# A hybrid decoder layer on one core: the float32 products inside a scan chunk, issued by two column halves of the stationary block

## The chip, the cores and the metric

The kernel runs on one core of one Trainium2 chip. The metric is the device time of one execution in microseconds. Before the change it is 1580.88 us, the median of three runs (1580.54 to 1581.92). The input is float32 and the output must agree with a float32 reference, so nearly all large products are done as three float32r products of a high and a low part (in the code `mm3` and `steps3`), and some small ones directly in float32.

## The reference, cut to what matters

One layer over 1024 tokens with 1024 channels: RMSNorm, one input projection, then two token mixers side by side (differential attention with 8 heads, and a Mamba-2 scan, "SSD", with 32 heads in 4 groups of 8), gates, three output projections. The change is in the scan. Its chunked form, with chunks of L = 128 tokens, is

```
a_cum = cumsum(dt * A)                                   # per chunk and head
seg   = a_t[..., :, None] - a_t[..., None, :]
decay = exp(where(causal, seg, -inf))                    # l x s, zero for s > l
cb    = einsum('bclgn,bcsgn->bcgls', Cc, Bc)
y_diag = einsum('bcgjls,bcsgjp->bclgjp', cb[:, :, :, None] * decay, xdt)
...
y_off = einsum('bclgn,bcgjpn->bclgjp', Cc, prev) * exp(a_cum)[..., None]
y = (y_diag + y_off) ...
```

`y_diag` is the product in question: for each chunk (8), each group (4) and each head in the group (8) a 128 x 128 block `cb * decay` (l by s) times a 128 x 64 block `xdt` (s by head channel). That is 32 chunks-and-groups, with 8 small products each.

## The kernel before, in words

The program is written out by a planner. Generators (one per piece of work: a head's projection, an attention block, a scan chunk) are run by `Plan.run` in the order in which the planner's clock `pl.t` says that they are due; each emitted instruction moves that clock or an engine's clock by a modelled cost. `pl.t` is the clock of TensorE: `mm` (line 207) emits one matmul and adds its cost, `tp` (line 216) a transpose. So the order in which instructions stand on each engine's queue follows from those costs. Nothing is moved afterwards: the kernel is compiled with a manual schedule. Loads and stores all go through SyncE's queue (`load`, line 262).

The stages on TensorE, in order of time: the normalised input and the front projections with conv and gates (to about 580 us, the scan of group 0 and the start of group 1 among them), attention heads with their projections `pma`, scores `sc`, transposes `pa`, value products `av`, and the rest of the scan woven in, with the last gates `pg` behind them (to about 1276 us), then the output projections, which use a Strassen-like scheme on sums of blocks (`pz`, `py`, `px` with `wp`, and `fYc`, `fXc`, `fZc` in the front; the final `po..`).

One scan chunk is `ssd_chunk(g, c, ...)`, line 1506. In the parts that matter:

- `ab` is a 128 x 8 x 128 tile: for the 8 heads of the group the block decay, transposed (partition is s, column is l). `load_ab` (line 1477) loads the cumulated exponents by one DMA, masks them on GpSimd (line 1482) and exponentiates on ScalarE, eight instructions. There is one such buffer.
- `pc` is the 128 x 128 product of B and C (`cb`), line 1547. VectorE multiplies `ab` by it, line 1623.
- `xdt` is x times dt, made on GpSimd.
- `pO` holds the off-diagonal part in PSUM, made by three float32r products (line 1578) and scaled in place by VectorE; in the first chunk of a group there is none, and the tile is called `pD`.
- The loop at line 1640 then does the 8 products with `ab[:, j, :]` as the stationary operand and 64 columns of `xdt` as the moving one, accumulating onto `pO` (or writing `pD`).
- Then VectorE adds the skip term, multiplies by the gate, and so on to the store of the chunk's output.

A float32 product that is not a transpose stands in the trace as two pairs of a weight load and a matmul: the 8 products of a chunk are 16 weight loads (PEld) and 16 matmuls (PE). In this text these 16 pairs of one chunk are called a burst; there are 32 of them, 28 written to `pO` and 4 to `pD`.

Of the kernel before, what the change touches and what calls it, by code (L numbers as in the profile page):

```python
# [15 lines left out]
P = 128  # L16
# [129 lines left out]
def tile_hybrid_layer(ctx: ExitStack, tc: tile.TileContext, x, norm_w, w_in, q_norm_w, k_norm_w,  # L146
# [40 lines left out]
    def midt(shape=(P, 512), dt=F32, name="m"):  # L187
        return mid.tile(list(shape), dt, tag="b2", name=name)
# [7 lines left out]
    def trt(name):  # L196
        return ps_tr.tile([P, 512], F32, tag="tr", name=name)
# [9 lines left out]
    def mm(o, lhsT, rhs, start, stop, after=0.0, **kw):  # L207
        nc.tensor.matmul(o, lhsT=lhsT, rhs=rhs, start=start, stop=stop, **kw)  # L208
        n, m = rhs.free_size(), lhsT.free_size()
        if rhs.dtype == F32:  # L210
            c = max(4 * n / 2400, 0.215)
        else:
            c = max(n / 2400 + lag[0], 0.057 if m <= 64 else 0.107)
        pl.t = max(pl.t, after) + c
# [8 lines left out]
    def mm3(o, ah, al, bh, bl, first, last):  # L223
        mm(o, ah, bh, first, False)
        mm(o, ah, bl, False, False)
        mm(o, al, bh, False, last)
# [1245 lines left out]
    def ssd_core(g):  # L1472
        state = {"st": {}, "pre": {}, "n": 0, "did": set()}
        ssd_n[g] = state
        abs_ = {}

        def load_ab(c):
            k = yield from pl.get(abb)
            ab = bigt([P, GH, P], name=f"ab{g}{c}")
            t = load(ab, act_d[c, g * GH:(g + 1) * GH, :].partition_broadcast(P)) + 1.0  # L1480
            yield t
            nc.gpsimd.affine_select(out=ab, in_=ab, pattern=[[0, GH], [1, P]], compare_op=ALU.is_ge, fill=-1e30,  # L1482
                                    base=0, channel_multiplier=-1)
            t = pl.op("G", 1.06, t, True)
            yield t
            for j in range(GH):
                t = act(ab[:, j, :], ab[:, j, :], AF.Exp, t - HOP, bias=nac[:, c, g * GH + j:g * GH + j + 1])
            abs_[c] = (ab, k, t)
        need = [(b, h) for b in [16 + g, 20 + g] + list(range(g * 4, g * 4 + 4)) for h in range(2)]
        while any(cv_at.get(i, INF) > pl.t for i in need) or any(z_at.get((g, t), INF) > pl.t for t in range(NT)):  # L1490
            yield pl.t + 0.5
        pl.spawn(load_ab(0))
        for c in range(NT):
            if c + 1 < NT:
                pl.spawn(load_ab(c + 1))
            while c - state["n"] >= 2 or c and c - 1 not in state["did"]:
                yield pl.t + 0.2
            pl.spawn(ssd_chunk(g, c, state, abs_))
            yield pl.t + (PACE if bigs.avail(3) <= pl.t or 'setup' in ready else SLOW)
# [6 lines left out]
    def ssd_chunk(g, c, state, abs_):  # L1506
# [19 lines left out]
        kxdt, xdt = kxr, midt(name=f"xdt{g}{c}")  # L1526
# [93 lines left out]
        ab, kab, t_ab = abs_.pop(c)  # L1620
# [13 lines left out]
        if c:  # L1634
            pD, k, t1 = cell
            yield max(t1, pl.t)
        else:
            k = yield from pl.get(trs, first=True)
            pD = trt(f"pD{g}{c}")
        for j in range(GH):  # L1640
            mm(pD[:, j * 64:(j + 1) * 64], ab[:, j, :], xdt[:, j * 64:(j + 1) * 64], c == 0, True,
               skip_group_check=True)
        abb.give(kab, pl.t + 0.1)
        at = max(pe_done(), t_n)
        yield at
# [583 lines left out]
```

## Time and profile before

| | |
|---|---|
| median of three runs | 1580.88 us (1580.54 to 1581.92) |
| profiled execution: time | 1580.41 us |
| profiled execution: span from first to last instruction | 1578.7 us |
| TensorE busy, matmul / weight load | 1553.7 us (98%) / 1299.0 us (82%) |
| VectorE, ScalarE, GpSimd busy | 75%, 60%, 50% |
| mean granted TensorE clock | 0.998 |
| first and last burst of the kind that is changed | 310.4 us, 1073.7 us (first matmul) |

PE is the matmul side of TensorE, PEld its weight-load side. [...] In a row of a timeline the columns are the start, the length from the first start to the last end, the engine, line, operation, tiles, shapes and the count of merged records. "128\*64" is the stationary block, rows by columns; "128x512 f32" the moving operand. The 1.7 us between the span and the execution's time lie around the first and the last instruction.

### The profile page before, as it was taken

How to read it: one execution, taken by the hardware profiler on the slowest of the kernel's cores; microseconds unless marked ns; L12 is line 12 of the kernel's file. 1: busy time of each engine (PE TensorE's matmuls, PEld its weight loads, DVE VectorE, ACT ScalarE, POOL GpSimd, SP SyncE). 2: the span in 40 equal slices, each digit the busy share in tenths (PEclk: the TensorE clock that was granted, in tenths of full speed). 3: DMA queues.
4: the chain of work that ended last, by engine and by line, in shares of the span. 5: the costliest groups of instructions: out<-in, count | busy, mean ns of one | idle time of the engine just before them, and what ended most of it. 6: DMA issues, size and time to landing. Idle time of an engine off the chain costs nothing.

```text
span 1578.7 us, 24834 instructions
## 1 busy us (share of the span) xinstructions
PE 1553.7 (98%) x7858; PEld 1299.0 (82%) x7858; DVE 1183.6 (75%) x2143; ACT 939.4 (60%) x2273; POOL 785.3 (50%) x906
## 2 busy tenths in 40 slices
PE   7999999999999999999999999999999999999999
PEld 5777888888888888888888888888888888888887
DVE  6778867568787778767778787877556687898985
ACT  7653434467565576778677777776666554443350
POOL 3274465345555554546574846454756745332005
PEclk9999999999999999999999999999999999999999
DMA  6576698744454552424373522333336697798846
GB/s 227 162 250 194 230 301 284 247 153 139 133 150 157 151 158 96 134 62 122 111 236 122 152 89 81 110 112 118 107 134 224 193 366 253 267 323 273 302 140 220
DMA packets 254821, 287.38 MB, mean 182 GB/s; under 512 B 18391, under 2 KB 162528, under 8 KB 254690
## 3 DMA queue, kind: packets, MB, share of 16 engines
q1 hardware_dynamic: 254686, 285.79, 55.7%
q8 instruction: 62, 1.02, 0.3%
q14 instruction: 69, 0.57, 0.1%
q10 hardware_dynamic: 4, 0.00, 0.0%
HBM read 196.47 MB, written 89.26 MB: 181 GB/s over the span
## 4 chain that ended last, share of the span: by engine, by line
PE 85%; ACT 3%; DVE 3%; DMA 3%; POOL 3%; issue 2%; SPq 0%; POOLq 0%; DVEq 0%; ACTq 0%
PE pma L208 19%; PE pz L208 11%; PE py L208 5%; PE fYc L208 5%; PE sc L208 4%; PE pO L208 4%; PE av L208 4%; PE fXc L208 3%; PE fZc L208 3%; PE px L208 3%; PE fYg L208 3%; PE pg L208 2%; PE pmz L208 2%; PE pa L217 2%; PE poz L208 1%
## 5 line engine op out<-in xcount | busy, mean ns | idle before, releaser
L208 PE MATMUL pma<-w,hH 128*128 128x512 f32 x1024 | 343.8, 404 | 0.0
L208 PEld LDWEIGHTS pma<-w,hH 128*128 128x128 f32 x1024 | 187.7, 189 | 32.9 <-DVE xdt L242 0.2
L208 PE MATMUL pma<-w,hL 128*128 128x512 f32 x512 | 205.7, 402 | 0.0
L234 ACT ACTIVATE w<-raw 128x512 fp32r<-128x512 f32 (+1 forms) x166 | 101.3, 629 | 56.0 <-DMA raw<-wf_d 21.7
L242 DVE TENSOR_TENSOR w<-raw,w 128x512 fp32r<-128x512 f32 (+1 forms) x134 | 107.1, 817 | 27.0 <-ACT w L234 24.1
L234 ACT ACTIVATE p<-p,nm 128x256 f32<-128x256 f32 (+7 forms) x128 | 98.8, 774 | 33.8 <-DVE nm L916 33.3
L208 PEld LDWEIGHTS pma<-w,hL 128*128 128x128 f32 x512 | 96.5, 188 | 16.6
L242 POOL TENSOR_TENSOR rawf<-rawf,rawf 128x512 f32<-128x512 f32 x54 | 71.8, 1330 | 75.1 <-DVE wp L242 30.5
L208 PE MATMUL fYc<-ft,wp 128*128 128x512 f32 x432 | 106.5, 392 | 2.4 <-DVE ft L242 1.8
L208 PEld LDWEIGHTS fYc<-ft,wp 128*128 128x128 f32 x432 | 80.3, 188 | 20.2 <-DVE ft L242 2.2
L208 PE MATMUL pz<-w,ft 128*128 128x512 f32 x384 | 90.1, 391 | 0.9 <-DVE w L242 0.9
L234 ACT ACTIVATE wp<-rawp 128x512 fp32r<-128x512 f32 x72 | 44.1, 627 | 78.4 <-POOL rawp L242 25.6
L242 POOL TENSOR_TENSOR os<-os,os 128x512 f32<-128x512 f32 x48 | 66.9, 1393 | 36.4 <-DMA os<-in_w_in_dram 14.8
L208 PEld LDWEIGHTS pz<-w,ft 128*128 128x128 f32 x384 | 71.7, 188 | 16.0 <-DVE w L242 1.3
L242 POOL TENSOR_TENSOR rawp<-rawp,rawp 128x512 f32<-128x512 f32 x36 | 54.4, 1521 | 54.2 <-DVE wp L242 50.2
L234 ACT ACTIVATE ab<-ab,nac 128x128 f32<-128x128 f32 x256 | 78.5, 397 | 3.5 <-POOL ab L1482 3.4
L916 DVE CUSTOM_DVE_ANT_0 p<-sc,maskb 128x512 f32<-128x512 f32 (+3 forms) x128 | 72.4, 584 | 6.6 <-PE sc L208 6.0
L274 POOL TENSOR_TENSOR rs<-rs,mhalf 128x4 f32<-128x4 f32 (+1 forms) x71 | 72.8, 1025 | 5.9
L208 PE MATMUL av<-v,at 128*128 128x128 f32 x576 | 75.2, 275 | 0.0
L208 PEld LDWEIGHTS av<-v,at 128*128 128x128 f32 x576 | 72.5, 191 | 3.2
L234 ACT ACTIVATE wp<-rawf 128x512 fp32r<-128x512 f32 x100 | 60.5, 624 | 17.5 <-POOL rawf L242 16.3
L948 POOL TENSOR_TENSOR rec<-s,mone 128x1 f32<-128x1 f32 x64 | 37.2, 583 | 63.7 <-ACT p L234 62.5
(376 smaller groups left out, 4410.3 us busy)
## 6 DMA issues: line engine op xcount, KB each, us to landing
raw<-in_w_in_dram SPq DMA_DIRECT2D x104, 256.0 KB, 3.2
rawf<-in_w_in_dram SPq DMA_DIRECT2D x72, 256.0 KB, 4.7
ab<-act_d SPq DMA_DIRECT2D x32, 512.0 KB, 4.7
wf_d<-os SPq DMA_DIRECT2D x48, 256.0 KB, 5.1
cv_d<-cv SPq DMA_DIRECT2D x48, 256.0 KB, 2.9
raw<-wf_d SPq DMA_DIRECT2D x48, 256.0 KB, 3.3
t_d<-ts SPq DMA_DIRECT2D x24, 512.0 KB, 4.0
os<-in_w_in_dram SPq DMA_DIRECT2D x32, 256.0 KB, 3.8
```

Of the source, the lines that this page charges most:

```text
L208: nc.tensor.matmul(o, lhsT=lhsT, rhs=rhs, start=start, stop=stop, **kw)
L217: nc.tensor.transpose(out=o, in_=i, identity=ident if idn is None else idn)
L234: nc.scalar.activation(o, i, f, **kw)
L242: (nc.vector if eng == "V" else nc.gpsimd).tensor_tensor(out=o, in0=a, in1=b, op=op)
L274: nc.gpsimd.tensor_tensor(out=dst, in0=dst, in1=mhalf[:, 0:cols], op=ALU.pow)
L916: nc.vector.tensor_tensor_reduce(out=p[:, j:e], in0=sc[i][:, 0:e - j], in1=maskb[:, S - n + j:S - n + e], scale=-1.0, scalar=nms[i - 1] if ...
L948: nc.gpsimd.tensor_tensor(out=rec, in0=sums[1], in1=mone, op=ALU.pow)
```

## The change

Each head's 128 x 128 block goes to TensorE as two blocks of 128 x 64: columns 0 to 63 (the first 64 tokens of the chunk), whose result goes to PSUM partitions 0 to 63, and columns 64 to 127, whose result goes to partitions 64 to 127 of the same columns. The moving operand is the same 64 columns of `xdt` for both. Nothing is left out: the zero quarter of the first half (s > l) is still multiplied. In the built program each half occupies its own half of the array's columns: the first is placed at column 0, the second at column 64, each with a size of 128 rows by 64 columns. The planner's cost of a float32 product with a stationary block of at most 64 columns becomes 0.108 us, where a full one of 64 moving columns costs 0.215.

```
         n, m = rhs.free_size(), lhsT.free_size()
         if rhs.dtype == F32:
-            c = max(4 * n / 2400, 0.215)
+            c = max(4 * n / 2400, 0.215) if m > 64 else 0.108
         else:
...
         for j in range(GH):
-            mm(pD[:, j * 64:(j + 1) * 64], ab[:, j, :], xdt[:, j * 64:(j + 1) * 64], c == 0, True,
-               skip_group_check=True)
+            js = slice(j * 64, (j + 1) * 64)
+            for ls in (slice(0, 64), slice(64, P)):
+                mm(pD[ls, js], ab[:, j, ls], xdt[:, js], c == 0, True, skip_group_check=True)
```

The order on TensorE around the first burst of the program (group 0, chunk 0; `pz` is a product of the front's z projection), with the rows of before and of the change marked by - and +:

```order
 L208 MATMUL pz_2987<-w_2814,ft_335 128x512
 L208 MATMUL pz_2987<-w_2830,ft_333 128x512 x2
-L208 MATMUL pD_2996<-xdt_2855,ab_2795 128x64 x8
+L208 MATMUL pD_2996<-xdt_2855,ab_2795 64x64 x16
 L208 MATMUL pz_2987<-w_2830,ft_335 128x512
 L208 MATMUL pz_2987<-w_2868,ft_334 128x512 x2
```

Eight products become sixteen, each with an output of 64 partitions by 64 columns; the neighbours are the same. So it is at all 24 bursts of groups 0 to 2, and the other rows of TensorE stand as before up to 896 us in the trace of before (the transposes `py26` of group 2, chunk 6).

The planner's clock for a burst moves from 8 x 0.215 = 1.720 to 16 x 0.108 = 1.728 us. From there on that is enough to let work fall due in another order. TensorE before, around the first burst of group 3 (`pD30`; `pma43` is a projection of head 4, token block 3; `px31` is the next chunk's transposes):

```order
L217 MATMUL px31_10080<-ident_99,xr31_10012 128x128 x4
L208 MATMUL pma43_10067<-w117_9664,hH_114 128x512 x2
L208 MATMUL pma43_10067<-w117_9664,hL_115 128x512
L208 MATMUL pma43_10067<-w118_9696,hH_114 128x512 x2
L208 MATMUL pma43_10067<-w118_9696,hL_115 128x512
L208 MATMUL pma43_10067<-w119_9713,hH_114 128x512 x2
L208 MATMUL pma43_10067<-w119_9713,hL_115 128x512
L208 MATMUL pma43_10067<-w120_9727,hH_114 128x512 x2
L208 MATMUL pma43_10067<-w120_9727,hL_115 128x512
L208 MATMUL pma43_10067<-w121_9757,hH_114 128x512 x2
L208 MATMUL pD30_10122<-xdt30_9846,ab30_9848 128x64 x8
```

and in the changed program:

```order
L208 MATMUL pma42_10164<-w117_9848,hL_115 128x512
L208 MATMUL pma42_10164<-w118_9883,hH_114 128x512 x2
L208 MATMUL pma42_10164<-w118_9883,hL_115 128x512
L208 MATMUL pma42_10164<-w119_9895,hH_114 128x512 x2
L208 MATMUL pD30_10211<-xdt30_10047,ab30_10049 64x64 x16
L208 MATMUL sc3500_10236<-kk30_8702,qh31_10085 128x512
L208 MATMUL sc3500_10236<-kk30_8702,qlo1_5659 128x512
```

The burst has moved ahead of the rest of `pma42`, of a score block and of the beginning of `pma43`. On SyncE's queue the load of its `ab30` moved the other way, behind one weight load and one store:

```order
L263 DMA zc27_9812<-z_d_90 128x512
L263 DMA ab30_9848<-act_d_87 128x1024
L263 DMA raw126_9856<-in_w_in_dram 128x4x128
L263 DMA ya_d_84<-yt30_9670 128x512
L263 DMA raw127_9878<-in_w_in_dram 128x4x128
```

```order
L263 DMA zc27_10003<-z_d_90 128x512
L263 DMA raw126_10033<-in_w_in_dram 128x4x128
L263 DMA ya_d_84<-yt30_9854 128x512
L263 DMA ab30_10049<-act_d_87 128x1024
L263 DMA raw127_10063<-in_w_in_dram 128x4x128
```

The first is before, the second the changed program. To the end of the attention (1276 us) some rows of every engine change places in the same way; the work itself is the same.

## The prediction

> **What bounds the kernel now.** I read the page first, for the engine that sets the end, and then the stages in which the changed products stand.
>
> ```profile
> span 1578.7 us, 24834 instructions
> PE 1553.7 (98%) x7858; PEld 1299.0 (82%) x7858; DVE 1183.6 (75%) x2143; ACT 939.4 (60%) x2273; POOL 785.3 (50%) x906
> PE 85%; ACT 3%; DVE 3%; DMA 3%; POOL 3%; issue 2%; SPq 0%; POOLq 0%; DVEq 0%; ACTq 0%
> ```
>
> TensorE is busy 98% of the span and makes 85% of the chain of waits. The table by stage shows where it is full:
>
> ```profile
> 300.00:600.00 300.00, 296.95 (x1426) 1.00 0.49 151
> 600.00:880.00 280.00, 278.83 (x1632) 1.00 0.40 125
> 880.00:1080.00 200.00, 199.40 (x1175) 1.00 0.38 118
> 896.00:1276.00 380.00, 379.03 (x2137) 1.00 0.44 142
> ```
>
> The second number is TensorE's busy time; from 300 to 1080 us, where all 32 bursts stand, it is idle for 3.05 + 1.17 + 0.60 us. So what a burst costs TensorE goes to the end one for one, and what another engine gains or loses there does not. The clock is full (1.00) and cannot give anything.
>
> A burst, by the records of its tile (the four `pD` bursts have the same durations):
>
> ```profile
> L208 PEld LDWEIGHTS pO<-xdt,ab x448: 186/192/247, 346.7 to 1075.3; 128*128 128x128 f32 x150
> L208 PE MATMUL pO<-xdt,ab x448: 217/275/323, 346.9 to 1075.3; 128*128 128x64 f32 x150
> ```
>
> Records overlap, so the cost is in the distances. The timelines of the first burst's loads, and of one burst with its neighbours (matmuls, then loads):
>
> ```profile
> 310.37 1.86 PEld L208 LDWEIGHTS pD<-xdt,ab 128*128 128x128 f32 x16 [0.26 <-issue]
> ...
> 602.92 0.39 PE L208 MATMUL pma<-w,hH 128*128 128x512 f32 x1
> 603.15 0.33 PE L208 MATMUL pO<-xdt,ab 128*128 128x64 f32 x2
> ...
> 605.17 0.39 PE L208 MATMUL pma<-w,hH 128*128 128x512 f32 x1
> ...
> 602.92 1.98 PEld L208 LDWEIGHTS pO<-xdt,ab 128*128 128x128 f32 x16
> 604.82 0.19 PEld L208 LDWEIGHTS pma<-w,hL 128*128 128x128 f32 x1
> ```
>
> Three readings. The sixteen loads of the first burst take 1.86 us of which the last record is 0.19: (1.86 - 0.19) / 15 = 0.111 us from load to load. The first two matmuls stand 0.33 - 0.275 = 0.055 us apart: their streaming is half as long as a load, so **the burst is bound by its weight loads**. And the first load begins at 602.92, with the start of the `pma` matmul ahead of it, so it is hidden, while the load of the `pma` behind the burst is not. From the `pma` at 602.92 to the one at 605.17 are 2.25 us, with two 512-column products (0.23 us each, 602.92 to 603.15) and the burst in them: 2.25 - 0.46 = 1.79 us. That is 16 x 0.112: 15 loads of its own, and that of its follower.
>
> **The change, part by part.** It removes 16 full loads per burst and adds 32 of half the columns; 16 matmuls of 64 moving columns become 32 of 64. No DMA, no instruction of another engine is added.
>
> The half load. No row of before has a float32 load of 128 x 64, but there are half and quarter blocks in the small dt projection (in float32r), with the full one for comparison:
>
> ```profile
> L208 PEld LDWEIGHTS pdt<-hH,w x16: 133/134/138, 115.6 to 122.7; 128*64 128x64 f32 x16
> L208 PEld LDWEIGHTS pdt<-hL,w x16: 107/108/108, 115.8 to 122.5; 128*32 128x32 f32 x16
> L208 PEld LDWEIGHTS pma<-w,hH 128*128 128x128 f32 x1024 | 187.7, 189 | 32.9 <-DVE xdt L242 0.2
> ```
>
> 188 to 134 to 108 ns for 128, 64 and 32 columns: 54 ns less for the first 64 columns, 26 for the next 32. A load's time goes with its columns, on a fixed latency. Taken off the pitch, a half load is 112 - 54 = 58 ns from start to start. The other near row is the only stream of short products, eight transposes of 64 moving columns:
>
> ```profile
> L217 PEld LDWEIGHTS ptdt<-ident,dtraw x8: 134/138/140, 124.4 to 124.8; 64*128 64x128 f32 x8
> ...
> 124.40 0.57 PEld L217 LDWEIGHTS ptdt<-ident,dtraw 64*128 64x128 f32 x8 [0.37 <-DVE dtraw L259]
> 125.04 0.30 PEld L208 LDWEIGHTS fXc<-hH,wp 128*128 128x128 f32 x2
> ```
>
> Their load records are about as long as the half load's (138 against 134), and they stand (0.57 - 0.14) / 7 = 0.061 us apart. So TensorE can be fed a pair every 0.061 us; faster than that this row does not show it. The lower end is the streaming, 55 ns, below which a single file of matmuls can't go. I take 58, with 55 and 62 as the ends: it comes from loads of the same shape, the 61 from transposes.
>
> The sum for a burst, in single file: the first load is hidden as before; then 31 half loads, then the follower's full load: 31 x 0.058 + 0.112 = 1.910 us, against 1.79: +0.118 us. Over 32 bursts +3.8 us. With 55 it is 1.817, +0.8 us in all; with 62, 2.034, +7.8 us. Twice as many loads of half the length bring nothing in themselves, and each load brings its gap of some 4 ns between matmul and load once more.
>
> The planner's cost: 16 x 0.108 against 8 x 0.215, 8 ns of plan per burst. Up to 896 us the order is untouched; from there to 1276 us rows change places. TensorE is idle for 0.97 us in these 380 us (fourth row of the table), so a better order can bring at most 1 us. The place where a loss is in sight is the first burst of group 3, which now stands ahead of a score block while the load of `ab30` stands behind a weight load and a store on SyncE's queue. In the trace of before, in the window from 900 to 930 us:
>
> ```profile
> L234 ACT ACTIVATE ab<-ab,nac x12: 385/387/388, 899.7 to 914.7; 128x128 f32<-128x128 f32 x12
> L242 DVE TENSOR_TENSOR ab<-ab,pc x2: 1211/1216/1222, 901.1 to 925.5; 128x1024 f32<-128x1024 f32 x2
> ```
>
> `ab30` is exponentiated by 915.1 us and its VectorE product starts only at 925.5, so some 10 us of slack cover a burst that comes earlier. If the cover is gone, what waits is everything behind the burst on TensorE. I put the order at 0, with -1 and, by the 3 us that the stage from 300 to 600 loses to such waits in all, +3.
>
> Behind the burst VectorE adds the skip term to `pO`; it gets it 0.1 us later. Nothing on TensorE is waiting for that until the transposes `py` at the chunk's end, and the 1.2 and 0.6 us of idle time in the table say that these waits have room.
>
> **Sum:** 1580.41 us (the profiled execution: its span of 1578.7 and 1.7 us around it) + 3.8 = 1584.2. The median of the runs is 0.47 above the profiled execution; against it I say **1584.6 us**.
>
> **The rivals.**
>
> *The two halves run side by side.* The halves sit in different columns of the array and write different partitions. If loads and matmuls of one half go on while the other half's are under way, two pairs take the time of one: 29 ns per pair. A burst is then 31 x 0.029 + 0.112 = 1.011 us, -0.78; over 32, -25 us: **1556**. For it: the array is used by halves, and the operands are disjoint. Against it: in the trace loads keep single file. Each begins only when the matmul ahead of it has begun (602.92 and 602.92 in the rows above), and in the new order a half's two pairs, high and low, still follow each other before the other half comes. [...]
>
> *Changing the array's form drains it.* Behind the eight `ptdt` transposes, whose blocks have 64 rows, the next load should start 0.06 us after the last one at 124.40 + 0.57 - 0.14 = 124.83; it starts at 125.04, 0.15 us late. If a burst of half columns pays this at entry (where the first half load, 0.06 us, is then not hidden either) and at exit, it is +0.36 us per burst, +11.5 in all: **1596**. Against it: the dt projection switches between blocks of 128, 64 and 32 columns at full pace:
>
> ```profile
> 115.55 0.39 PE L208 MATMUL pe<-hH,w 128*128 128x512 f32 x1
> 115.78 0.39 PE L208 MATMUL pdt<-hH,w 128*64 128x512 f32 x1
> 116.00 0.63 PE L208 MATMUL pdt<-hL,w 128*32 128x512 f32 x2
> 116.47 0.40 PE L208 MATMUL pdt<-hH,w 128*64 128x512 f32 x1
> ```
>
> 0.22 to 0.24 us from start to start, as between full blocks. But these are float32r and all at column 0. [...]
>
> *Nothing changes.* If a load to the other half needn't wait for the matmul ahead, the gaps vanish and the streaming's 55 ns bounds: +0.8 us, **1581**.
>
> That the halves are loaded as full blocks all the same would cost 16 x 0.112 more per burst, +57 us; the 134 ns against 188 speak against it, and I give it nothing.
>
> **How the numbers follow.** Single file 0.40, side by side 0.29, drained 0.17, no change 0.14. A measurement of this kernel can tell about 0.2%, 3.2 us, from no change. Side by side is faster, and a lucky order adds 0.02 to it: 0.31. Drained is slower. Single file runs from +0.8 to +7.8 us and lies on both sides of the bound, 0.27 slower and 0.13 same; with the rest of the no-change case, same is 0.25 and slower 0.44. The likeliest case alone would be 1581 to 1589. As cases of both signs hold much of the chance, the range reaches from 1555, the side-by-side case with 1 us of better order, to 1595, which leaves out the upper part of the drained one.
>
> **What would show it.** In the changed profile: load records of about 134 ns on `pO` and `pD`, 1,024 of them; their pitch in a burst, 58 to 62 ns for single file, 55 for no change, about 30 for side by side; the first load of a burst starting with the matmul ahead of it, and the follower's within 0.12 us of the last, or 0.15 us later for a drain; from 300 to 1080 us TensorE as full as before. Right for a wrong reason would be a time near 1584 with a pitch of 30 ns and drains that eat it, or with bursts as before and 4 us of waits between 896 and 1276 us.

## The result and the profile after

The changed kernel takes **1571.03 us** (median; 1569.45 to 1571.73) beside 1581.4 us (1580.54 to 1582.65) for the kernel before: a ratio of 0.9932, 95% interval 0.9915 to 0.995. It is 0.7% faster. The forecast was 1584.6 us, slower, so its sign was wrong. The time lies inside the range of 1555 to 1595 us, between the "side by side" rival's number and the kernel before; that is no merit of the sum, since the range was drawn to hold cases of both signs.

From the page of the changed kernel, the span, the engines and the chain of waits:

```profile
span 1567.7 us, 25852 instructions
PE 1537.3 (98%) x8370; PEld 1270.4 (81%) x8370; DVE 1185.2 (76%) x2143; ACT 939.2 (60%) x2273; POOL 782.7 (50%) x906
PE 83%; ACT 5%; DVE 3%; POOL 3%; DMA 3%; issue 2%; SPq 0%; DVEq 0%; POOLq 0%; ACTq 0%
```

TensorE was busy for 1553.7 us and is now for 1537.3: -16.4 us. The span fell by 11.0, so TensorE's idle time rose, from 25.0 to 30.4 us. Two things happened, then. The records of the tile `pO`, and one burst with its neighbours, matmuls first and then loads:

```profile
L208 PEld LDWEIGHTS pO<-xdt,ab x896: 132/138/138, 344.3 to 1053.8; 128*64 128x64 f32 x180
L208 PE MATMUL pO<-xdt,ab x896: 222/222/271, 344.3 to 1053.9; 128*64 128x64 f32 x180
```

```profile
595.29 0.39 PE L208 MATMUL pma<-w,hH 128*128 128x512 f32 x1
595.61 1.15 PE L208 MATMUL pO<-xdt,ab 128*64 128x64 f32 x32
596.70 0.50 PE L208 MATMUL pma<-w,hL 128*128 128x512 f32 x1
597.03 0.39 PE L208 MATMUL pma<-w,hH 128*128 128x512 f32 x1
...
595.61 1.01 PEld L208 LDWEIGHTS pO<-xdt,ab 128*64 128x64 f32 x32 [0.35 <-issue]
596.69 0.19 PEld L208 LDWEIGHTS pma<-w,hL 128*128 128x128 f32 x1
```

The loads are as long as expected (138 ns at the median; 134 was taken from the dt projection). But 32 of them fit into 1.01 - 0.14 = 0.87 us: 28 ns each. Their starts in the trace, in ns from the first, show how:

```
   0   7 | 55  62 | 111 118 | 169 176 | 228 234 | 286 293 | 344 351 | ...
```

Two loads start 7 ns apart, one for each half, and the next two some 58 ns later. **Each half runs in a file of its own, at the 58 ns that were forecast for one file, and the two files run beside each other.** The trace doesn't say to which half a load belongs; the kernel with both halves in one place, below, shows that the pairs are one of each. From here on a place is the part of the array's columns in which a block stands, with the PSUM partitions that its result goes to, and the form of a block is its width: full, half or quarter.

The second reading is at the ends. The burst's first load stands with its own first matmul (595.61 and 595.61), not with the `pma` ahead of it as before: it isn't hidden, and the burst begins 595.61 - 595.29 = 0.32 us after that `pma` where 0.23 is the pace. The last of the 32 matmuls starts 1.15 - 0.22 = 0.93 us after the first, at 596.54; the follower's load starts 0.15 us behind that. From `pma` to `pma`, less two 512-column products: 597.03 - 595.29 - 0.46 = **1.28 us** for a burst, where it was 1.79. Over 32 bursts that is -16.3 us, all of what TensorE's busy time lost.

The table by stage shows where the 5.3 us of new idle time are (30.35 less 25.04, before rounding; second number of a row: TensorE's busy time). The first two rows are the changed kernel's, the third is the kernel before:

```profile
600.00:880.00 280.00, 277.30 (x1872) 1.00 0.40 127
880.00:1290.00 410.00, 403.20 (x2401) 1.00 0.48 155
```

```profile
880.00:1290.00 410.00, 409.03 (x2293) 1.00 0.45 149
```

The longer waits of the changed kernel between 880 and 1290 us say for what (us in total, times, longest):

```profile
PE sc L208 <- DVE kk L242: 1.7, 2, 1.4
PE py L217 <- ACT xn L234: 1.6, 2, 1.5
PE pma L208 <- ACT yt L234: 1.1, 1, 1.1
PE pa L217 <- DVE p L250: 1.0, 2, 0.6
```

From 880 to 1290 us, the part with the new order of rows, TensorE is idle for 6.8 us, where it was idle for 1.0. From 600 to 880, where the order is the old one, it is idle for 2.7 us, 1.5 more than before: there the bursts are faster and what follows them is not always ready. In the rest of the program it is idle for 2 us less than before.

### The profile page after: what moved, and what is told of

Read it like the earlier page. It is cut to its first block, busy times and chain, and to the rows that moved or that the text cites. A ratio compares the mean times of both kernels' runs of the same rounds, so it can differ in the third digit from the quotient of the medians.

```text
span 1567.7 us, 25852 instructions
## 1 busy us (share of the span) xinstructions
PE 1537.3 (98%) x8370; PEld 1270.4 (81%) x8370; DVE 1185.2 (76%) x2143; ACT 939.2 (60%) x2273; POOL 782.7 (50%) x906
## 4 chain that ended last, share of the span: by engine, by line
PE 83%; ACT 5%; DVE 3%; POOL 3%; DMA 3%; issue 2%; SPq 0%; DVEq 0%; POOLq 0%; ACTq 0%
PE pma L208 16%; PE pz L208 11%; PE py L208 6%; PE fYc L208 5%; PE sc L208 4%; PE px L208 4%; PE av L208 4%; PE fXc L208 4%; PE fZc L208 3%; PE fYg L208 3%; PE pO L208 3%; PE pg L208 2%; PE pmz L208 2%; DMA raw<-in_w_in_dram 2%; PE pa L217 2%
## 5 line engine op out<-in xcount | busy, mean ns | idle before, releaser
L242 DVE TENSOR_TENSOR w<-raw,w 128x512 fp32r<-128x512 f32 (+1 forms) x134 | 103.6, 792 | 25.4 <-ACT w L234 22.9
L234 ACT ACTIVATE p<-p,nm 128x128 f32<-128x128 f32 (+7 forms) x128 | 98.8, 774 | 33.4 <-DVE nm L916 31.5
```

Source lines behind the costliest of these rows:

```text
L234: nc.scalar.activation(o, i, f, **kw)
L242: (nc.vector if eng == "V" else nc.gpsimd).tensor_tensor(out=o, in0=a, in1=b, op=op)
```

## The experiments

Theory A, after the result: the halves run side by side in two places of the array; each burst pays for the change of form on its way in and out; and the new order of rows costs some 5 us by itself. Rivals: two loads in flight anywhere make the gain, not the two places; the lost time at the ends belongs to the burst's waits; the order is innocent and the idle time comes from faster bursts.

### The halves in the old order, and the full blocks in the new

The planner's cost of a half product is what moved the rows. Set so that a burst is planned at 1.720 us as before, the halves stand in the old order:

```diff
-            c = max(4 * n / 2400, 0.215) if m > 64 else 0.108
+            c = max(4 * n / 2400, 0.215) if m > 64 else 0.1075
```

> The half blocks, but with the planner's cost of a half at 0.1075 us instead of 0.108 (16 x 0.1075 = 8 x 0.215), so that every instruction of every engine stands in the order of the kernel before; only the bursts differ. Theory A (a burst is 0.51 us shorter, 1.79 to 1.28, and the new order gives 5 us of it back in waits): 32 x 0.51 = 16.3 us less than before, about 1565 us, and TensorE's idle time at the 25.0 us of before. Rival B (the waits come because TensorE arrives earlier everywhere, whatever the order): about 1571 us, as the changed kernel, with 30 us of idle time.

And the full blocks of the kernel before, planned at 8 x 0.216 = 1.728 us, stand in the new order:

```diff
-            c = max(4 * n / 2400, 0.215)
+            c = max(4 * n / 2400, 0.216 if n == 64 else 0.215)
```

> Full blocks as before, with the planner's cost of such a product at 0.216 us (8 x 0.216 = 16 x 0.108), so that every instruction stands in the order of the changed kernel. Theory A (the new order costs about 5 us by itself): about 1586 us. Rival B (the order costs nothing): 1581 us, within 1 us.

Measured: halves in the old order **1566.13 us** (ratio to before 0.9901, 0.9885 to 0.9917), better than both kernels (its interval and the changed kernel's just touch); full blocks in the new order 1589.59 us (1.0047, 1.0031 to 1.0064). Span and engines from the page, and the stage from 880 us from the table by stage, of the first kernel and then of the second:

```profile
span 1562.3 us, 25860 instructions
PE 1537.2 (98%) x8370; PEld 1271.8 (81%) x8370; DVE 1181.1 (76%) x2143; ACT 939.0 (60%) x2273; POOL 785.2 (50%) x906
```

```profile
880.00:1290.00 410.00, 407.99 (x2432) 1.00 0.48 157
```

```profile
span 1588.1 us, 24826 instructions
PE 1556.3 (98%) x7858; PEld 1298.6 (82%) x7858; DVE 1189.2 (75%) x2143; ACT 939.8 (59%) x2273; POOL 785.1 (49%) x906
```

```profile
880.00:1290.00 410.00, 403.02 (x2258) 1.00 0.45 144
```

In the old order the halves have the same busy time (1537.2) and idle time of 25.1 us, that of the kernel before; the full blocks in the new order are idle for 7.0 us from 880 to 1290, as the changed kernel is for 6.8. So edit and order are two separate things: the halves bring 16.5 us of TensorE's time, and the order takes time back, with or without them: some 5 us with halves (1571.03 against 1566.13), and 7 to 8 us with full blocks (ratio 1.0047; its interval reaches from 5 to 10 us, so that this is more than 5 is not shown). Not all that the full blocks' profile loses belongs to the order: 1.6 us of it are a wait of `px` for its DMA at 297 us, ahead of every row that moved, and TensorE's busy time is 2.6 us higher than before, for which no cause was found. That faster bursts make TensorE wait more does not explain the 5 us: in the old order the idle time as a whole is what it was.

### Both halves in one place

In the 28 `pO` bursts the second half goes to the first half's columns and partitions too, so that only one place of the array is used; instructions, loads and order are those of the changed kernel.

```diff
-                mm(pD[ls, js], ab[:, j, ls], xdt[:, js], c == 0, True, skip_group_check=True)
+                mm(pD[slice(0, 64) if c else ls, js], ab[:, j, ls], xdt[:, js], c == 0, True, skip_group_check=True)
```

> The changed kernel, but in the 28 bursts on pO both halves write partitions 0 to 63, so that both stand at column 0 of the array; the second half's sums land on the first half's, and partitions 64 to 127 get no inner product. Same count and size of loads and matmuls, same order. Theory A (the gain comes from two places of the array working at the same time): pairs in single file at 58 ns, a burst of 1.28 + 31 x 0.028 = 2.15 us, 28 x 0.87 = 24 us more than the changed kernel, about 1595 us. Rival C (half blocks are quicker by themselves, for instance by a second set of weight buffers that any half can use): pitch 30 ns, about 1571 us.

Measured: 1596.15 us (1593.68 to 1598.61; ratio 1.0091). The burst with its neighbours in the timeline, matmuls and then the load behind it:

```profile
605.95 0.61 PE L208 MATMUL pma<-w,hH 128*128 128x512 f32 x2
606.49 2.08 PE L208 MATMUL pO<-xdt,ab 128*64 128x64 f32 x32
608.50 0.50 PE L208 MATMUL pma<-w,hL 128*128 128x512 f32 x1
608.83 0.39 PE L208 MATMUL pma<-w,hH 128*128 128x512 f32 x1
...
608.50 0.19 PEld L208 LDWEIGHTS pma<-w,hL 128*128 128x128 f32 x1
```

(2.08 - 0.22) / 31 = 0.060 us from matmul to matmul: single file, with the same gaps at the ends: the load behind the burst starts at 608.50, 0.15 us after the last matmul (606.49 + 1.86 = 608.35). The burst costs 2.20 us. This is the forecast's single file (1.910 us) with 0.29 us more, the way in and out, and it shows that the gain comes from the second place: 60 ns a pair without it, 30 with it. Columns and PSUM partitions were moved together, and this run doesn't tell them apart. That both halves add to the same sums here is not what holds them up: in the next kernel the blocks of eight heads, each with sums of its own, stand 58 ns apart within one place as well.

### First halves of all heads, then second halves

```diff
-        for j in range(GH):
-            js = slice(j * 64, (j + 1) * 64)
-            for ls in (slice(0, 64), slice(64, P)):
+        for ls in (slice(0, 64), slice(64, P)):
+            for j in range(GH):
+                js = slice(j * 64, (j + 1) * 64)
```

> The changed kernel with the loop turned round: the first halves of all 8 heads, then the second halves of all 8. Same instructions, same result. Theory A1 (the two places overlap only where their pairs stand next to each other in the queue): 58 ns from pair to pair in both parts, +28 us, about 1598 us. Theory A2 (each place takes its own work out of the queue, as far ahead as 16 pairs): pitch 30 ns as before, about 1571 us. Something between would say how far ahead it looks.

Measured: 1594.67 us (1590.74 to 1598.6; ratio 1.0081). A burst, and the starts of its loads around the passage from the first halves to the second, in ns:

```profile
607.45 1.90 PE L208 MATMUL pO<-xdt,ab 128*64 128x64 f32 x32
```

```
first halves    577  635  694  752      809       865
second halves                      754      810        869  923  981 ...
```

The second half's first load waits until the first half's fourteenth is under way, and then runs beside the rest. (Which half a start belongs to is read from the spacing.) So in this order two places were not enough: the instructions for the other place did not stand close behind. The overlap is worth 58 ns for each of some three pairs (1.68 us from first to last matmul against 1.86 in one place).

### Four heads' first halves, then their second halves

```diff
-        for j in range(GH):
+        for j, ls in [(j + i, ls) for j in range(0, GH, 4) for ls in (slice(0, 64), slice(64, P)) for i in range(4)]:
             js = slice(j * 64, (j + 1) * 64)
-            for ls in (slice(0, 64), slice(64, P)):
-                mm(pD[ls, js], ab[:, j, ls], xdt[:, js], c == 0, True, skip_group_check=True)
+            mm(pD[ls, js], ab[:, j, ls], xdt[:, js], c == 0, True, skip_group_check=True)
```

> Half blocks as in the changed kernel, in the order: first halves of heads 0 to 3, second halves of heads 0 to 3, then the same for heads 4 to 7; all other rows as in the changed kernel. How far ahead does TensorE reach for a pair of the other column half? Theory (a few pairs: with all 16 pairs of one half ahead of the 16 of the other, only the last 3 ran beside the other half): three passages of 8 pairs to 8 pairs, each with 3 side by side, so 32 - 9 = 23 steps of 58 ns, 1.28 us from first to last matmul against 0.93 now, 32 x 0.35 = +11 us, about 1582 us. Rival (it reaches 8 pairs or more ahead, and the earlier run was held by something else): 16 to 20 steps, 0.93 to 1.10 us, +0 to +5.5 us, 1571 to 1577 us. No look-ahead at all: 32 steps, 1.80 us, +28 us, 1599 us.

Measured: 1584.56 us (1.0027, 1.0014 to 1.0039), 1.32 us from first to last matmul where 1.28 was expected:

```profile
598.76 1.54 PE L208 MATMUL pO<-xdt,ab 128*64 128x64 f32 x32
```

At each of the three passages the new half's first load starts 1 to 2 ns after the old half's sixth of eight, when the sixth pair's matmul and two further pairs wait. In this run and the one before TensorE passed five waiting instructions of one place to reach the other (six with the load that starts 1 to 2 ns ahead), and not more.

### Full and half blocks mixed

Four heads of each burst keep full blocks. In one kernel they alternate with halved heads, in the other the four full ones come first; the order of all other rows is the changed kernel's, for which the planner's cost of a full block is set to 0.216 us.

```diff
-            for ls in (slice(0, 64), slice(64, P)):
+            for ls in (slice(0, 64), slice(64, P)) if j % 2 else (slice(0, P),):
```

```diff
-            for ls in (slice(0, 64), slice(64, P)):
+            for ls in (slice(0, 64), slice(64, P)) if j > 3 else (slice(0, P),):
```

> Heads 0, 2, 4, 6 of each burst stay full blocks and heads 1, 3, 5, 7 are halved; the order of all rows is that of the changed kernel. Which part of the burst is paid for a change of form? Theory (each change between full and half blocks is paid, 0.09 us on the way in and 0.15 us on the way out, with the first load uncovered, together some 0.27 us for one in-and-out, as the entry and exit of the changed kernel's bursts show): 8 full pairs at 0.112 plus 16 half pairs at 0.029 plus four in-and-outs at 0.27 = 0.90 + 0.46 + 1.08 = 2.44 us for each burst against 1.28 now, so 32 x 1.16 = +37 us, about 1608 us; the timeline shows four gaps of 0.15 us within a burst. Rival (the 0.27 us belong to the burst's own start and end, its waits for ab and xdt and what follows it, and not to the form): 0.90 + 0.46 + 0.27 = 1.63 us, 32 x 0.35 = +11 us, about 1582 us, and no gap within a burst.

> Heads 0 to 3 of each burst stay full blocks and heads 4 to 7 are halved; order of the rows as in the changed kernel. The same number of full and half blocks as with alternate heads, and one change of form in and one out for each burst. Theory (a change of form is what is paid): 0.90 + 0.46 + 0.27 = 1.63 us for each burst, 32 x 0.35 = +11 us over the changed kernel's 1571, about 1582 us, 26 us less than alternate heads; the gap on the way in moves from the burst's start to its middle, and the burst's own first load is hidden again. Rival (the start of a burst is what is paid): the same 1582 us, but as much as alternate heads, and the late start stays at the first load of the burst.

Measured: alternating 1608.73 us (1.0171, 1.015 to 1.0192), four and four 1584.43 us (1.0014, 1.0003 to 1.0026). A burst's loads with those of its neighbours, alternating and then four and four:

```profile
607.29 0.41 PEld L208 LDWEIGHTS pma<-w,hH 128*128 128x128 f32 x2
607.74 2.57 PEld L208 LDWEIGHTS pO<-xdt,ab 128*128 128x128 f32 x24
610.38 0.19 PEld L208 LDWEIGHTS pma<-w,hL 128*128 128x128 f32 x1
```

```profile
601.28 0.19 PEld L208 LDWEIGHTS pma<-w,hH 128*128 128x128 f32 x1
601.51 1.70 PEld L208 LDWEIGHTS pO<-xdt,ab 128*128 128x128 f32 x24
603.28 0.19 PEld L208 LDWEIGHTS pma<-w,hL 128*128 128x128 f32 x1
```

The same 24 loads take 2.57 us with four changes in and out, and 1.70 with one. (2.57 - 1.70) / 3 = 0.29 us for one in-and-out, where 0.27 was expected. And where a burst begins with full blocks, its first load starts 0.23 us behind the `pma` load ahead, hidden as before. So it is the change of form that is paid, wherever it stands, and not the burst's start.

### Quarters

```diff
-            for ls in (slice(0, 64), slice(64, P)):
+            for ls in [slice(i, i + 32) for i in range(0, P, 32)]:
```

with the planner's cost halved for it, so that all other rows stand in the order before.

> Each head's decay block as four stationary blocks of 32 columns in place of two of 64, every other row in the order of the kernel before. Theory (a column place of its own runs beside the others, each at its own pitch, which goes with its columns: 112 ns for 128, 58 for 64, so about 31 for 32): four places at once give 16 x 31 = 0.50 us for a burst against 0.93 now, and the passage in and out stays at 0.27 us and an uncovered load: 32 x 0.43 = 14 us below the halves in the same order (1566), about 1552 us. Rival one (TensorE holds two places at once, or reaches only two pairs ahead): two at 31 ns, 0.99 us, 1566 to 1568 us, no change. Rival two (the start of a pair costs a fixed time, some 30 ns whatever the place, since 30 ns is the mean pitch of the halves): 64 x 30 = 1.92 us, 32 x 0.99 = +32 us, about 1598 us.

Measured: 1568.78 us (0.9917, 0.99 to 0.9934), no better than the halves in that order. None of the three cases is quite right:

```profile
L208 PEld LDWEIGHTS pO<-xdt,ab x1792: 105/110/111, 349.5 to 1064.7; 128*32 128x32 f32 x200
...
602.65 1.10 PE L208 MATMUL pO<-xdt,ab 128*32 128x64 f32 x64
```

```
matmul starts:  248 255 262 268 | 303 310 317 323 | 359 367 373 380 | 415 422 428 435 | ...
```

Four pairs do start within 20 ns of each other, in four places. But the next four come 55 ns later, not 31: the 55 ns at which two matmuls of 64 moving columns already stood behind each other in the kernel before. So a place with half blocks went at the pitch expected of its loads (58 ns), and one with quarters at 55 ns, which fits the streaming of 64 columns; other numbers of moving columns were not tried. A burst still takes 16 x 55 = 0.88 us against 0.93, and its whole cost is 1.23 us against 1.28. The 1.6 us that this should bring are not seen in the time: TensorE's idle time is 30.9 us where the halves have 25.1, and its busy time is no lower (1537.9 against 1537.2 us). A row of the quarters' waits and two of their windows say where the gain went:

```profile
PE px L217 <- DMA xr<-cv_d: 3.6, 2, 2.0
```

```profile
298.00:300.00 2.00, 1.98 (x8) 0.61 1.05 392
300.00:302.00 2.00, 2.00 (x7) 0.53 0.87 299
```

Twice `px` waits for its DMA, for 3.6 us, which it does not do in the profile of the halves. The first of these waits, 2.0 us at 296 us, lies ahead of the first burst, and behind it the granted clock (the number behind the count) is 0.61 and 0.53, which costs 2.00 x (0.39 + 0.47) = 1.7 us of work at full clock. The edit had changed nothing before that wait, and the same one stands in the profiles of the full blocks in the new order, of both halves in one place and of the first halves of all heads, but not in the others. Kernels with the same rows up to there have it and don't have it, so it doesn't follow from the edit. The profile thus doesn't speak against the 1.6 us; the runs scatter by more than that and can't show them.

### Other planner costs

The measured cost of a burst is 1.28 us, 0.08 for a half product; the planner was told 0.108. Three more values, 0.08, 0.085 and 0.1, give three more orders of the same instructions.

```diff
-            c = max(4 * n / 2400, 0.215) if m > 64 else 0.108
+            c = max(4 * n / 2400, 0.215) if m > 64 else 0.08
```

> Half blocks as in the changed kernel; the planner is told 0.08 us for a half product (1.28 us measured for a burst of 16) where the changed kernel says 0.108 and the kernel in the old order 0.1075, so its order of rows is a third one. Theory (the order by itself is worth several us either way, and it is chance which one the planner falls into): TensorE's busy time stays at 1537 us, its idle time lies between the 25 us of the old order and 32 of the new one, 1562 to 1575 us. Rival (the planner places work better when its cost is right, so its idle time falls below 25 us): below 1562 us.

> Half blocks as in the changed kernel, with 0.085 us as the planner's cost for a half product, a fourth order of rows. Theory (the time scatters with the order and does not follow the cost): anywhere between 1562 and 1597 us, TensorE busy from 1537 us with idle time from 25 to 48 us. Rival (a smaller cost makes the planner ask for data too early, so the time rises as the cost falls): between 1571 us at 0.108 and 1597 us at 0.08, close to the latter, 1590 to 1597 us.

> Half blocks as in the changed kernel, with 0.1 us as the planner's cost for a half product, a fifth order of rows. Theory (the time scatters with the order): 1562 to 1597 us, not between its neighbours by rule. Rival (the time rises as the cost falls, from 1571 us at 0.108 to 1597 us at 0.08): 1576 to 1581 us.

Measured: 0.08: 1597.21 us (1.0094, 1.0079 to 1.011); 0.085: 1584.60 us (1.0026, 1.0011 to 1.0042); 0.1: 1584.77 us (1.003, 1.0018 to 1.0043). The true cost gives the slowest of the five orders. The spans and engines of the three, in that order:

```profile
span 1598.4 us, 25859 instructions
PE 1550.3 (97%) x8370; PEld 1279.5 (80%) x8370; DVE 1174.5 (73%) x2143; ACT 940.6 (59%) x2273; POOL 777.7 (49%) x906
```

```profile
span 1583.4 us, 25850 instructions
PE 1545.4 (98%) x8370; PEld 1275.1 (81%) x8370; DVE 1177.3 (74%) x2143; ACT 942.8 (60%) x2275; POOL 778.2 (49%) x906
```

```profile
span 1582.9 us, 25842 instructions
PE 1542.1 (97%) x8370; PEld 1273.7 (80%) x8370; DVE 1184.0 (75%) x2143; ACT 944.6 (60%) x2275; POOL 789.7 (50%) x906
```

Against my expectation TensorE's busy time did not stay at 1537 us. The timeline of the 0.08 kernel, its table of 2 us windows and a row of its waits show why:

```profile
436.89 1.52 PE L208 MATMUL fYg<-ft,wp 128*128 128x512 f32 x6
440.65 1.81 PE L208 MATMUL pO<-xdt,ab 128*64 128x64 f32 x32 [2.23 <-DVE ab L242]
442.39 2.52 PE L208 MATMUL fYg<-ft,wp 128*128 128x512 f32 x6
```

```profile
438.00:440.00 2.00, 0.42 (x2) 1.00 0.92 263
440.00:442.00 2.00, 1.35 (x29) 0.72 1.00 304
442.00:444.00 2.00, 2.00 (x13) 0.50 0.33 64
444.00:446.00 2.00, 2.00 (x10) 0.92 0.63 229
```

```profile
PE pO L208 <- DVE ab L242: 5.5, 4, 2.7
```

This burst, placed 2.23 us before its `ab` block is ready, costs those 2.23 us, and then the granted clock (the number behind the count) is 0.72, 0.50 and 0.92 in the next windows: six 512-column products take 2.52 us where they took 1.52. What the clock takes is 2.00 x (0.28 + 0.50 + 0.08) = 1.7 us, so this wait is paid nearly twice. Not every long wait is: behind one of 2.74 us in the same kernel, 599.51 to 602.25 us, the clock stayed full.

```profile
600.00:602.00 2.00, 0.00 (x0) 1.00 0.72 205
602.00:604.00 2.00, 1.75 (x35) 1.00 0.11 45
```

Over the whole program the mean granted clock of the 0.08 kernel is 0.991, where the halves in the old order have 0.999: 0.008 x 1600 = 13 us, about the 13.1 us by which TensorE's busy time is higher. With 0.085 and 0.1 it is 0.996 and 0.997, some 5 and 3 us of the 8.2 and 4.9 that their busy times rose. In sum TensorE waits 5.5 us for `ab` in the 0.08 kernel, and 4.7 and 5.5 in the two others; in the changed kernel that wait isn't among the longer ones. Why the planner's order is worse with a truer cost was not tried; its other costs and due times were left as they are. The rise with the falling cost missed both of its ranges (1590 to 1597 and 1576 to 1581 us, where 1584.6 and 1584.8 were measured). The scatter's range held both, but it was so wide that this says little. What is settled is that the order of the same instructions moves the time from 1566 to 1597 us, about twice what the edit itself is worth.

## Why the prediction was wrong, and where it was right

- **What bounds the kernel: right.** TensorE sets the end. What a burst lost came off TensorE's busy time one for one (-16.3 us by bursts, -16.4 by the page), and in the old order off the span too (1578.7 to 1562.3).
- **The half load: right, in a place.** 58 ns from start to start, with 138 ns records; 55 and 62 were the ends.
- **Single file: the step that failed.** The sum took 31 x 58 ns for a burst, and so 0.118 us more than before. The halves made two files, the burst's matmuls stand 30 ns apart, and a burst costs 0.51 us less. The argument against it was that in the trace each load began only when the matmul ahead had begun, and that a half's two pairs follow each other before the other half comes. But before, all blocks were in one place, and that row could not speak for two. And the high and low pair of a half only have to be passed: in the kernels that group the halves, by eight heads and by four, TensorE passed a matmul and two pairs. Moved to one place, the same instructions do run in single file (60 ns, 1596.15 us).
- **The rival "side by side": right in its mechanism.** The pairs stand 30 ns apart in two places against 60 in one; grouping by halves lost most of it (1.68 us from first to last matmul, against 0.93 for the changed kernel and 1.86 in one place). Its chance of 0.29 was an estimate of mine: nothing in the trace of before shows two places at work. The rival's 1556 us was 15 us too low, by the ways in and out (32 x 0.27 = 8.6 us) and the order (some 5 us), which it left out.
- **The rival "drain": paid as well.** I gave the two as alternatives. The changed kernel's bursts show 0.15 us at the exit, as behind the `ptdt` transposes before, and 0.09 more than the pace at the entry; the alternating heads show 0.29 us for each in-and-out. That TensorE drains in that time is not shown, only that the next start comes late. The forecast price was 0.15 + 0.15 + 0.06 = 0.36 us; the burst is 0.27 us above the 1.01 of the rival "side by side", of which 0.03 are the pitch (30 ns, not 29). What I held against it, that the dt projection changes form at full pace, is not explained by these runs. That the projection uses one place alone is not the reason, since the float32 halves in one place pay the same 0.15 us; it also differs in type (float32r) and in the length of its matmuls (512 columns), which no run here separates.
- **The order: mis-sized.** It was put at 0 with bounds of -1 and +3 us; it is about +5 with halves, +7 to +8 with full blocks. The idle time that a stage has now bounds what a new order can gain, and was used rightly for that. It does not bound what it can lose. The one risk named, the slack of `ab30`, held; other waits (`kk`, `xn`, `yt`, `p`) took its place.
- **The sum, mended:** 1580.4 - 16.3 + 5.3 = 1569.4 us, the profiled execution's 1569.45. The 16.3 are counted from the bursts, but the 5.3 are the idle time of this same profile, so this is bookkeeping. With the order's price from the other kernels (1571.03 - 1566.13 = 4.9) it is 1569.0.

## What to carry to other kernels

Short float32 products that are bound by weight loads, as these are, can gain from two half-width stationary blocks in different columns, if the two halves' instructions alternate within a few pairs (grouped by four heads a burst took 1.32 us from first to last matmul, where it took 0.93 with the halves of each head in turn), and if one stretch holds enough of them to pay about 0.27 us for its way in and out: here sixteen pairs went from 1.79 to 1.28 us. Where a planner orders the rows, keep its order fixed while an edit is measured, since a change of 0.5 ns in a planned cost was worth 5 us here, and then try orders apart. An observation that instructions run one behind the other holds for the resources they shared in that trace, and not for others.

## What the runs showed of the hardware

- In the changed kernel two column halves ran fully beside each other, 7 ns apart, each at its own 58 ns, 30 ns a pair; in one place the same pairs stood 60 ns apart. Four quarters ran beside each other too, 20 ns from the first to the fourth, each at 55 ns, as two matmuls of 64 moving columns stood in the kernel before.
- A stretch of half blocks started 0.32 us after the product ahead of it, 0.09 us more than the pace of its neighbours (0.23), and the full block's load behind it 0.15 us after its last matmul, with two places or one; with full blocks on both sides each way in and out cost 0.29 us.
- In the kernel that issues the first halves of all heads ahead of the second, the second half's first load, told by the spacing, started at 754 ns, ahead of five waiting instructions of the first half: its fourteenth matmul, at 807 ns, and two pairs. In the kernel that goes by four heads it was again a matmul and two pairs.
- After a wait of 2.23 us in the kernel with 0.08 the granted clock was 0.72, 0.50 and 0.92 in the next windows of 2 us (1.7 us lost); after one of 2.74 us in the same kernel it stayed at 1.00. After one of 2.0 us in the kernel with quarters it was 0.61 and 0.53 (1.7 us lost).
